# Feed-forward of a hybrid encoder block: residual scaling moved into the first group's loop, last norm's sums taken with the additions and its squares summed by ScalarE

## The chip, the cores and the metric

One core of one Trainium2 chip runs the whole kernel. The metric is the device time of one execution in microseconds (us); lower is better. The engines are called by the profile's names: PE (TensorE matmul), DVE (VectorE), ACT (ScalarE), POOL (GpSimd), SP (SyncE, which issues most DMAs). Each has its own queue of instructions and works through it strictly in order.

## The reference, cut to what matters

```
x = layer_norm(x, ln_in)                       # x: 1024 frames x 1024 features, float32
m = sigmoid(gate_A) * gMLP(x) + sigmoid(gate_B) * RWKV7(x)
x = layer_norm(ALPHA * x + m @ w_o, ln1_g, ln1_b)
gate, val = split(x @ w_up)                    # 2688 columns each
h = gelu(causal_conv3(gate) + conv_b) * val
x = layer_norm(ALPHA * x + h @ w_down, ln2_g, ln2_b)
```

The change concerns the last line: the residual `ALPHA * x`, the additions of `h @ w_down` to it, and the mean and variance of the norm over each frame's 1024 features.

## The kernel before, in words

The kernel does the token mixer first (some 1257 us), then the feed-forward part that the change touches. Matrix products are made in a split form: each float32 operand is a high part (name ending in h) and a low part (ending in l), and `mm3` makes three matmuls of them. The low part of every weight is a subtraction on POOL, the high part a cast on ACT; the raw weight comes by a DMA on the SP queue.

The feed-forward part (from line 1083) runs over 21 blocks of 128 columns of `w_up`, in 7 groups `g` of three blocks `f`. For each block PE makes the gate product for two halves `h` of the frames (into PSUM tiles `pu`, two buffers) and the value product for both halves (into `ps`, two buffers). The weights are `fuh`/`ful` (gate), `wh`/`wl` (value) and `fdh`/`fdl` (w_down). ACT copies the gate product to `gb` and scales it into `t`; DVE adds two shifted terms of the convolution; ACT applies gelu; DVE multiplies by the value product and casts to `th`; POOL makes the low part `tl`. When the three blocks of a group are made, PE multiplies them with `w_down` (PSUM tiles `pd`, four buffers) for 8 row tiles `n` of 128 frames and two halves `j` of 512 features, and DVE adds each `pd` into the residual `acc[n][j]`. The 16 residual tiles lie in buffers left over from earlier stages, so they appear under many names: f, sht, tv, acc, bvs, ff, gams, in the order of `n` (f, f for n=0 and 1; f, sht for 2; tv 3; acc 4; bvs 5; ff 6; gams 7).

Before the first additions the residual must be scaled: `load_bc(2)` fetches the gain and the bias of the norm before, broadcast to all partitions (tiles `bf`), ACT multiplies both by ALPHA, and a loop over the 16 tiles multiplies by the first (all on DVE) and adds the second (even `n` on POOL, odd on DVE). The buffers `bf` are used again for the last norm's gain and bias, so that load (`load_bc(4)`, issued on the ACT queue) waits until the scaling is over.

In the last group `finish(n, bc)` follows the additions of each row tile: `ln_stats` (line 346) reads both halves with BATCH_NORM_STATS and aggregates them on DVE, `rstd_of` (line 339) takes a square root on ACT and a reciprocal on DVE, and then half 0 is normalised by two DVE instructions, half 1 by one on ACT and two on POOL; the result goes out by DMA. For the last row tile the cut lies at 832 of 1024 features instead of 512.

The order on each engine: the token mixer is recorded and ordered by the kernel's own planner (class `Weave`); its instructions show as L279. The feed-forward part is issued directly, through the recording wrapper (they show as L92), and there the framework's scheduler decides the order on each engine.

Of the kernel before, what the change touches and what calls it, by code (L numbers as in the profile page):

```python
# [8 lines left out]
F32 = mybir.dt.float32  # L9
F32R = mybir.dt.float32r  # L10
AF = mybir.ActivationFunctionType
ALU = mybir.AluOpType
AX = mybir.AxisListType

P = 128
D = 1024
S = 1024
HT = 512
KT = 8
# [3 lines left out]
NF = FF // P  # L23
GRP = 3
# [259 lines left out]
def hybrid_block(ctx: ExitStack, tc, x, w_in, w_v, pars, rows, bs, ws, lor, w_o, w_up, w_dn, out):  # L284
# [7 lines left out]
    tiny = W.enter(ctx, tc.tile_pool(name="tiny", bufs=3), 3)  # L292
# [46 lines left out]
    def rstd_of(var, eps, scale=1.0, n=1, tag="rs"):  # L339
        s = tiny.tile([P, n], F32, name="rs_s", tag=tag + "s")  # L340
        A.activation(s, var, AF.Sqrt, bias=eps, scale=scale)
        r = tiny.tile([P, n], F32, name="rs_r", tag=tag + "r")
        V.reciprocal(r, s)
        return r

    def ln_stats(src):
        st = tiny.tile([P, 2, 6], F32, name="ln_st")
        for q in range(2):
            V.bn_stats(st[:, q, :], src[q] if isinstance(src, list) else src[:, q * HT:(q + 1) * HT])
        mv = tiny.tile([P, 2], F32, name="ln_mv")  # L350
        V.bn_aggr(mv, st)
        return mv, rstd_of(mv[:, 1:2], eps_ln)
# [212 lines left out]
    acc = [None] * KT  # L565
# [518 lines left out]
    with ExitStack() as st:  # L1084
        ep = st.enter_context
        gp = ep(pool("gp", 1))
        fw = ep(pool("fw", 2))
        fs = ep(pool("fs", 2))
        hp = ep(pool("hp", GRP + 1))
        ps_u = ep(pool("ps_u", 2, PSUM))  # L1090
        ps_d = ep(pool("ps_d", 4, PSUM))

        def load2(src, nm, bufs):
            wr = fw.tile([P, D], F32, name="wr2")
            SY.dma_start(wr, src)
            wh = fw.tile([P, D], F32R, name=nm + "h", bufs=bufs)
            wl = fw.tile([P, D], F32R, name=nm + "l", bufs=bufs)
            split(wh, wl, wr)
            return wh, wl

        def up(w, h, own=False):
            return gemm(w, h, xs=x1k(), ps=ps_u.tile([P, HT], F32, name="pu") if own else None)

        def load_bc(i0):
            bc = [fs.tile([P, D], F32, name=f"bf{i}", bufs=1) for i in range(2)]
            for i in range(2):
                A.dma_start(bc[i], rows[i0 + i:i0 + i + 1, :].partition_broadcast(P))
            return bc

        def finish(n, bc):  # L1110
            mv, r = ln_stats(acc[n])
            nm = tiny.tile([P, 1], F32, name="ln_nm", tag="rss")
            V.scalar_tensor_tensor(nm, mv[:, 0:1], -1.0, r, ALU.mult, ALU.mult)
            cut = HT if n < KT - 1 else 832
            whole = gams.rearrange("p a c t -> p (a c t)")
            for j, js in enumerate((slice(0, cut), slice(cut, D))):
                aj = acc[n][j] if n < KT - 1 else whole[:, js]
                if j:
                    A.activation(aj, aj, AF.Identity, bias=nm, scale=r)
                    G.tensor_tensor(aj, aj, bc[0][:, js], ALU.mult)  # L1120
                    G.tensor_tensor(aj, aj, bc[1][:, js], ALU.add)
                else:
                    V.scalar_tensor_tensor(aj, aj, mv[:, 0:1], bc[0][:, js], ALU.subtract, ALU.mult)
                    V.scalar_tensor_tensor(aj, aj, r, bc[1][:, js], ALU.mult, ALU.add)
                SY.dma_start(out[n * P:(n + 1) * P, js], aj)

        for g in range(NF // GRP):
            hh, hl, wd = [], [], []
            for f in range(g * GRP, (g + 1) * GRP):
                wg = load2(w_up[f], "fu", 2) if f else w0[0]  # L1130
                wv = load_w(0, w_up[NF + f]) if f else w0[1]
                wd.append(load2(w_dn[f * P:(f + 1) * P, :], "fd", GRP))
                th = hp.tile([P, S], F32R, name="th")
                tl = hp.tile([P, S], F32R, name="tl")
                gb = gp.tile([P, S + P + 104], F32, name="gb")
                G.memset(gb[:, 0:2], 0.0)
                cw = lambda i: par[:, C_CW + i * NF + f:C_CW + i * NF + f + 1]
                ts = []
                for h in range(2):
                    pg = up(wg, h, True) if f or h else up0[0]  # L1140
                    A.copy(gb[:, 2 + h * HT:2 + (h + 1) * HT], pg)
                    t0 = fs.tile([P, HT], F32, name="t0", bufs=3)
                    A.activation(t0, pg, AF.Identity, bias=par[:, C_CB + f:C_CB + f + 1], scale=cw(2))
                    V.scalar_tensor_tensor(t0, gb[:, 1 + h * HT:1 + (h + 1) * HT], cw(1), t0, ALU.mult, ALU.add)
                    V.scalar_tensor_tensor(t0, gb[:, h * HT:(h + 1) * HT], cw(0), t0, ALU.mult, ALU.add)
                    A.activation(t0, t0, AF.Gelu)
                    ts.append(t0)
                for h in range(2):
                    hs = slice(h * HT, (h + 1) * HT)
                    pv = up(wv, h) if f or h else up0[1]  # L1150
                    V.tensor_tensor(ts[h], ts[h], pv, ALU.mult)
                    V.tensor_copy(th[:, hs], ts[h])
                    G.tensor_tensor(tl[:, hs], ts[h], th[:, hs].bitcast(F32), ALU.subtract)
                hh.append(th)
                hl.append(tl)
            if g == 0:
                bc = load_bc(2)
                for i in range(2):
                    A.mul(bc[i], bc[i], ALPHA)
                for n in range(KT):  # L1160
                    for j in range(2):
                        js = slice(j * HT, (j + 1) * HT)
                        V.tensor_tensor(acc[n][j], acc[n][j], bc[0][:, js], ALU.mult)
                        (V if n % 2 else G).tensor_tensor(acc[n][j], acc[n][j], bc[1][:, js], ALU.add)
            if g == NF // GRP - 1:
                bc = load_bc(4)
            for n in range(KT):
                ns = slice(n * P, (n + 1) * P)
                for j in range(2):
                    js = slice(j * HT, (j + 1) * HT)  # L1170
                    po = ps_d.tile([P, HT], F32, name="pd")
                    for i in range(GRP):
                        mm3(po, hh[i][:, ns], hl[i][:, ns], wd[i][0][:, js], wd[i][1][:, js], i == 0, i == GRP - 1)
                    V.tensor_tensor(acc[n][j], acc[n][j], po, ALU.add)
                if g == NF // GRP - 1:
                    finish(n, bc)
    st_m.close()


# [61 lines left out]
```

## Time and profile before

| what | us |
|---|---|
| median of 3 runs (1964.23 to 1970.06) | 1964.5 |
| the profiled execution: its own time | 1965.61 |
| the profiled execution: its span | 1963.8 |
| PE busy in the span | 1854.9 (94%) |
| DVE, ACT, POOL busy | 994.2 (51%), 857.2 (44%), 916.0 (47%) |
| the feed-forward part, from about 1257 to the end | about 707 |

The span runs from the first to the last instruction of the profiled execution; 1.8 us of its own time lie around it. Busy shares are means over the whole span; the change touches two short stretches of it, the first 50 us of the feed-forward part and the last 44 us, and these are read in their own rows. Times in rows are from the span's start.

### The profile page before, as it was taken

The page shows a single profiled execution, that of the slowest core. Times are in us where ns is not written, and L with a number is a line of the kernel's source. Part 1 is how long each engine was busy: PE and PEld are TensorE (multiplying, and loading weights), DVE is VectorE, ACT ScalarE, POOL GpSimd, SP SyncE. Part 2 cuts the span into 40 slices and gives each one's busy share as a digit, 9 for nine tenths or more (in the row PEclk, how much of TensorE's full clock was granted, in tenths as well). Part 3 has the DMA queues.
Part 4 walks back from the last instruction along what each step waited for, and adds up shares of the span by engine and source line. Part 5 has one row for each costly group of instructions (what it writes and reads, how often), then busy time and mean ns, then how long its engine had stood idle before and what let it go on. Part 6 is the DMA issues. An engine that isn't in the chain of part 4 may idle for free.

```text
span 1963.8 us, 27242 instructions
## 1 busy us (share of the span) xinstructions
PE 1854.9 (94%) x10024; PEld 1499.5 (76%) x10024; DVE 994.2 (51%) x1806; ACT 857.2 (44%) x1733; POOL 916.0 (47%) x1505
## 2 busy tenths in 40 slices
PE   6997899999999999999998899989999999999997
PEld 5996677677777777777776677768888888888886
DVE  8423745666555567555554467683333332333327
ACT  5544465655556566556565565421212121212121
POOL 5202575557656565675548662272423232323224
PEclk9998999999999999999998999999999999999999
DMA  6112121111112122112131322231111111111102
GB/s 211 33 49 61 46 64 58 52 46 47 55 52 68 55 54 63 38 58 65 47 93 55 97 86 62 79 115 44 54 43 55 42 55 42 57 41 58 39 1 86
DMA packets 78884, 119.13 MB, mean 61 GB/s; under 512 B 27776, under 2 KB 47488, under 8 KB 78752
## 3 DMA queue, kind: packets, MB, share of 16 engines
q1 hardware_dynamic: 60640, 96.94, 16.3%
q10 hardware_dynamic: 18112, 20.45, 3.2%
q8 instruction: 80, 1.31, 0.3%
q14 instruction: 52, 0.43, 0.1%
HBM read 103.08 MB, written 14.29 MB: 60 GB/s over the span
## 4 chain that ended last, share of the span: by engine, by line
PE 64%; POOL 17%; DVE 9%; issue 4%; ACT 3%; DMA 2%; ACTq 1%; POOLq 0%; SPq 0%; DVEq 0%
PE ps L279 17%; PE ps L92 11%; PE pu L92 11%; PE pd L92 10%; PE pp L279 8%; POOL ydx L279 6%; POOL tm L279 6%; PE pv L92 4%; PE pc L279 2%; POOL wl L279 2%; POOL ar L279 1%; PE py L279 1%; DVE ln_st L92 1%; DVE vl L92 1%; DVE f L92 1%
## 5 line engine op out<-in xcount | busy, mean ns | idle before, releaser
L279 PE MATMUL ps<-xh,wh 128*128 128x512 f32 x896 | 373.4, 417 | 33.2 <-DVE tkr L279 13.1
L279 PE MATMUL ps<-xh,wl 128*128 128x512 f32 x896 | 369.2, 413 | 6.6 <-POOL wl L279 6.3
L279 PE MATMUL ps<-xlo,wh 128*128 128x512 f32 x896 | 373.3, 417 | 0.0
L279 PEld LDWEIGHTS ps<-xh,wh 128*128 128x128 f32 x896 | 173.4, 194 | 66.3 <-DVE tkr L279 14.6
L279 PEld LDWEIGHTS ps<-xh,wl 128*128 128x128 f32 x896 | 173.0, 193 | 37.3 <-POOL wl L279 8.3
L279 POOL TENSOR_TENSOR tm<-ydx,bd 128x60 f32<-128x60 f32 (+24 forms) x496 | 167.3, 337 | 67.4 <-DMA bd<-a_d 12.4
L279 PEld LDWEIGHTS ps<-xlo,wh 128*128 128x128 f32 x896 | 173.2, 193 | 29.0 <-issue 1.0
L279 POOL TENSOR_TENSOR wl<-wr,wh 128x1024 fp32r<-128x1024 f32 x50 | 122.3, 2445 | 149.7 <-ACT wh L279 130.3
L92 DVE SCALAR_TENSOR_TENSOR t<-gb,par,t 128x512 f32<-128x512 f32 x84 | 89.6, 1067 | 193.4 <-ACT t L92 192.0
L279 POOL TENSOR_TENSOR ydx<-ydx,tm 128x60 f32<-128x60 f32 (+24 forms) x496 | 167.0, 337 | 37.2
L279 DVE SCALAR_TENSOR_TENSOR bs<-pc,gams,sgm 64x64 f32<-64x64 f32 x240 | 67.9, 283 | 161.5 <-PE pc L279 159.2
L92 POOL TENSOR_TENSOR fdl<-wr,fdh 128x1024 fp32r<-128x1024 f32 x21 | 51.4, 2463 | 196.4 <-ACT fdh L92 196.4
L92 PE MATMUL pd<-fdh,th 128*128 128x512 f32 x336 | 130.7, 389 | 0.0
L92 PE MATMUL pd<-fdl,th 128*128 128x512 f32 x336 | 130.7, 389 | 0.0
L92 PE MATMUL pd<-fdh,tl 128*128 128x512 f32 x336 | 130.7, 389 | 0.0
L92 ACT CAST fdh<-wr 128x1024 fp32r<-128x1024 f32 x21 | 21.5, 1051 | 196.5 <-PE pd L92 182.7
L92 POOL TENSOR_TENSOR wl<-wr,wh 128x1024 fp32r<-128x1024 f32 x22 | 56.3, 2560 | 63.6 <-ACT wh L92 63.6
L92 POOL TENSOR_TENSOR ful<-wr,fuh 128x1024 fp32r<-128x1024 f32 x20 | 48.7, 2437 | 78.7 <-ACT fuh L92 72.9
L279 PEld LDWEIGHTS pp<-ar,bd 64*128 64x128 f32 x512 | 61.8, 189 | 27.6 <-issue 17.8
L279 ACT ACTIVATE sgm<-bs,gams 128x128 f32<-128x128 f32 x128 | 51.4, 401 | 71.1 <-DVE bs L279 67.6
L92 POOL TENSOR_TENSOR tl<-t,th 128x512 fp32r<-128x512 f32 x42 | 55.6, 1325 | 56.2 <-DVE th L92 56.2
L279 PE MATMUL pp<-ar,bd 64*128 64x128 f32 x512 | 74.8, 288 | 6.1 <-DVE ar L279 4.7
(356 smaller groups left out, 4460.8 us busy)
## 6 DMA issues: line engine op xcount, KB each, us to landing
wr<-in_dram SPq DMA_DIRECT2D x113, 512.0 KB
bd<-a_d SPq DMA_DIRECT2D x64, 128.0 KB
vraw<-in_dram SPq DMA_DIRECT2D x8, 528.0 KB
xt<-in_dram SPq DMA_DIRECT2D x8, 512.0 KB
v_d<-xt ACTq DMA_DIRECT2D x8, 512.0 KB
fv<-v_d ACTq DMA_DIRECT2D x16, 256.0 KB
f<-q_d SPq DMA_DIRECT2D x32, 128.0 KB
m_d<-gu ACTq DMA_DIRECT2D x14, 256.0 KB
```

The costliest lines, as they stand in the source:

```text
L92: return fn(*a, **k)
L279: fn(*a, **k)
```

## The change

Three edits in the feed-forward part.

1. The scaling of the residual moves from one loop of its own into the loop over row tiles of group 0. The multiplications of even `n` go from DVE to POOL, and all additions go to POOL.
2. In the last group the addition of `pd` also writes each row's sum (`accum_out`), as a SCALAR_TENSOR_TENSOR instruction.
3. `finish` makes the mean from the two sums with small instructions on one column, lets ACT square the deviations of both halves with a sum beside (Square, bias = minus the mean, `accum_out`), adds the two sums on DVE, and takes `rstd` from that. The two BATCH_NORM_STATS and the aggregation per row tile are gone.

```
-        def finish(n, bc):
-            mv, r = ln_stats(acc[n])
-            nm = tiny.tile([P, 1], F32, name="ln_nm", tag="rss")
-            V.scalar_tensor_tensor(nm, mv[:, 0:1], -1.0, r, ALU.mult, ALU.mult)
+        def finish(n, bc, s):
+            st = tiny.tile([P, 6], F32, name="fst", tag="ln_st")
+            V.tensor_scalar(st[:, 0:1], s[:, 0:1], s[:, 1:2], -1.0 / D, ALU.add, ALU.mult)
+            V.tensor_scalar(st[:, 1:2], st[:, 0:1], -1.0, None, ALU.mult)
+            for j in range(2):
+                sq = fs.tile([P, HT], F32, name="t0", bufs=3)
+                A.activation(sq, acc[n][j], AF.Square, bias=st[:, 0:1], accum_out=st[:, 2 + j:3 + j])
+            V.tensor_tensor(st[:, 4:5], st[:, 2:3], st[:, 3:4], ALU.add)
+            r = rstd_of(st[:, 4:5], eps_ln, scale=1.0 / D)
+            nm, mv = st[:, 5:6], st[:, 1:2]
+            V.tensor_tensor(nm, st[:, 0:1], r, ALU.mult)
...
-                for n in range(KT):
-                    for j in range(2):
-                        js = slice(j * HT, (j + 1) * HT)
-                        V.tensor_tensor(acc[n][j], acc[n][j], bc[0][:, js], ALU.mult)
-                        (V if n % 2 else G).tensor_tensor(acc[n][j], acc[n][j], bc[1][:, js], ALU.add)
...
             for n in range(KT):
                 ns = slice(n * P, (n + 1) * P)
+                s = tiny.tile([P, 2], F32, name="fsum", tag="rss")
                 for j in range(2):
                     js = slice(j * HT, (j + 1) * HT)
+                    if g == 0:
+                        (V if n % 2 else G).tensor_tensor(acc[n][j], acc[n][j], bc[0][:, js], ALU.mult)
+                        G.tensor_tensor(acc[n][j], acc[n][j], bc[1][:, js], ALU.add)
...
-                    V.tensor_tensor(acc[n][j], acc[n][j], po, ALU.add)
+                    if g < NF // GRP - 1:
+                        V.tensor_tensor(acc[n][j], acc[n][j], po, ALU.add)
+                    else:
+                        V.scalar_tensor_tensor(acc[n][j], po, 1.0, acc[n][j], ALU.mult, ALU.add, accum_out=s[:, j:j + 1])
                 if g == NF // GRP - 1:
-                    finish(n, bc)
+                    finish(n, bc, s)
```

How the scheduler places this is not in the diff. **POOL at the start of group 0**, before, from the first scaling addition to `ful`, the low part of the gate weight of the second block (wr_12795 is the raw w_down weight of the first block, wr_12873 the raw gate weight of the second; bf_13153 is the scaled gain, bf_13154 the scaled bias):

```order
L92 TENSOR_TENSOR f<-f,bf_13154 128x512 x3
L92 TENSOR_TENSOR fdl<-wr_12795,fdh 128x1024
L92 TENSOR_TENSOR sht<-sht,bf_13154 128x512
L92 TENSOR_TENSOR tl<-t_12806,th 128x512
L92 TENSOR_TENSOR ful<-wr_12873,fuh 128x1024
```

and after the change, the same stretch:

```order
L92 TENSOR_TENSOR f<-f,bf_13153 128x512 x3
L92 TENSOR_TENSOR sht<-sht,bf_13153 128x512
L92 TENSOR_TENSOR acc_3713<-acc_3713,bf_13153 128x512
L92 TENSOR_TENSOR f<-f,bf_13154 128x512 x5
L92 TENSOR_TENSOR sht<-sht,bf_13154 128x512
L92 TENSOR_TENSOR tv<-tv,bf_13154 128x512 x2
L92 TENSOR_TENSOR acc_3713<-acc_3713,bf_13154 128x512
L92 TENSOR_TENSOR acc_3714<-acc_3714,bf_13153 128x512
L92 TENSOR_TENSOR fdl<-wr_12795,fdh 128x1024
L92 TENSOR_TENSOR tl<-t_12806,th 128x512
L92 TENSOR_TENSOR ful<-wr_12873,fuh 128x1024
```

Fifteen scaling instructions instead of four now stand ahead of `ful` on POOL.

**ACT in the same stretch**, as a piece of the difference (the two `bf` DMAs are the load of the last norm's rows; wr_13025 is the raw w_down weight of the third block):

```order
 L92 CAST fuh<-wr_13013 128x1024
 L92 ACTIVATE t_12837<-t_12837 128x512
-L92 CAST wh<-wr 128x1024
+L92 DMA bf_16815<-in_dram 128x1024
+L92 CAST wh<-wr 128x1024
+L92 DMA bf_16816<-in_dram 128x1024
 L92 CAST fdh<-wr_13025 128x1024
-L92 DMA bf_16767<-in_dram 128x1024
-L92 DMA bf_16768<-in_dram 128x1024
 L92 COPY gb<-pu 128x512
```

The two loads stand one and two places earlier; the copy of the second block's gate product (`gb`), which frees PSUM for PE, is still behind both and now also directly behind a cast that needs wr_13025.

**DVE in the last group**, one row tile (n=4, names acc_3713 and acc_3714), before:

```order
L92 TENSOR_TENSOR acc_3714<-acc_3714,pd 128x512
L92 SCALAR_TENSOR_TENSOR tv<-tv,rs_r,bf_16768 128x512
L92 BN_STATS ln_st<-acc_3714 128x6
L92 TENSOR_TENSOR bvs<-bvs,pd 128x512
L92 BN_AGGR ln_mv<-ln_st 128x2
L92 BN_STATS ln_st<-bvs 128x6
L92 RECIPROCAL rs_r<-rs_s 128x1
L92 SCALAR_TENSOR_TENSOR acc_3713<-acc_3713,ln_mv,bf_16767 128x512
L92 SCALAR_TENSOR_TENSOR ln_nm<-ln_mv,rs_r 128x1
```

and after:

```order
L92 SCALAR_TENSOR_TENSOR acc_3714,fsum<-pd,acc_3714 128x512
L92 TENSOR_TENSOR fst<-fst,rs_r 128x1
L92 SCALAR_TENSOR_TENSOR tv<-tv,rs_r,bf_16816 128x512
L92 TENSOR_SCALAR fst<-fsum 128x1
L92 TENSOR_SCALAR fst<-fst 128x1
L92 SCALAR_TENSOR_TENSOR acc_3713<-acc_3713,fst,bf_16815 128x512
L92 TENSOR_TENSOR fst<-fst 128x1
L92 SCALAR_TENSOR_TENSOR bvs,fsum<-pd,bvs 128x512
L92 RECIPROCAL rs_r<-rs_s 128x1
L92 SCALAR_TENSOR_TENSOR bvs,fsum<-pd,bvs 128x512
```

In the second list `TENSOR_TENSOR fst<-fst,rs_r` is the shift `nm` of the tile before, and `TENSOR_TENSOR fst<-fst` adds the two sums of squares; the additions of the next tile (`bvs,fsum<-pd,bvs`) stand behind it, where before one of them stood ahead of the aggregation.

## Rows read from the trace of the kernel before

**Rows 1.** The page's first section, and the busy time of each engine in two stretches of the feed-forward part (stretch, length, PE, PEld, DVE, ACT and POOL busy us with instructions, granted PE clock, DMA share, GB/s).

```profile
PE 1854.9 (94%) x10024; PEld 1499.5 (76%) x10024; DVE 994.2 (51%) x1806; ACT 857.2 (44%) x1733; POOL 916.0 (47%) x1505
...
1500.00:1600.00 100.00, 100.00 (x443) 82.81 (x442) 31.16 (x43) 20.99 (x28) 30.06 (x19) 1.00 0.17 53
1920.00:1964.00 44.00, 32.61 (x144) 26.66 (x143) 38.01 (x74) 8.62 (x16) 22.50 (x17) 0.92 0.26 96
```

**Rows 2.** Timeline of PE in group 0, around its two waits (start us, us, engine, line, what, in brackets the idle time before and what ended it).

```profile
1278.05 0.39 PE L92 MATMUL pu<-x1la,fuh 128*128 128x512 f32 x1
1280.67 0.50 PE L92 MATMUL pu<-x1ha,ful 128*128 128x512 f32 x1 [2.23 <-POOL ful L92]
...
1303.51 0.39 PE L92 MATMUL ps<-x1hb,wl 128*128 128x512 f32 x1
1308.89 0.79 PE L92 MATMUL pu<-x1ha,fuh 128*128 128x512 f32 x1 [4.99 <-ACT t L92]
```

**Rows 3.** Busy time by stretch again, columns as in rows 1: a stretch in the token mixer that begins 2.29 us after a wait of 7.49 us, and two stretches behind the first wait of rows 2.

```profile
1066.20:1069.70 3.50, 3.50 (x11) 2.71 (x10) 1.47 (x1) 0.00 (x0) 3.42 (x3) 0.50 0.44 150
...
1281.30:1284.70 3.40, 3.40 (x10) 2.67 (x9) 3.40 (x5) 0.53 (x1) 2.25 (x2) 0.52 0.51 154
1284.70:1288.10 3.40, 3.40 (x16) 2.76 (x15) 3.40 (x2) 0.52 (x1) 3.40 (x2) 0.98 0.07 11
```

**Rows 4.** The chain that ended last, the gate product of the third block of group 0 and of the first of group 1 (start us, us, what): 48 matmuls each.

```profile
1308.89 12.69 PE pu L92 x48
...
1365.10 10.88 PE pu L92 x48
```

**Rows 5.** Timeline of POOL in group 0: with DVE at work beside it, and from 1312 with DVE mostly waiting; last, a group of the same kind of 128x512 instruction with float32 output (count, busy us, mean ns).

```profile
1265.06 3.37 POOL L92 TENSOR_TENSOR f<-f,bf 128x512 f32<-128x512 f32 x2 [7.45 <-ACT bf L92]
1271.89 2.86 POOL L92 TENSOR_TENSOR fdl<-wr,fdh 128x1024 fp32r<-128x1024 f32 x1
1277.83 2.79 POOL L92 TENSOR_TENSOR ful<-wr,fuh 128x1024 fp32r<-128x1024 f32 x1
1312.21 2.40 POOL L92 TENSOR_TENSOR ful<-wr,fuh 128x1024 fp32r<-128x1024 f32 x1 [5.73 <-issue]
1317.08 1.30 POOL L92 TENSOR_TENSOR tl<-t,th 128x512 fp32r<-128x512 f32 x1 [0.89 <-DVE th L92]
1333.40 2.56 POOL L92 TENSOR_TENSOR wl<-wr,wh 128x1024 fp32r<-128x1024 f32 x1 [2.39 <-ACT wh L92]
...
L279 POOL TENSOR_TENSOR acc<-acc,bx 128x512 f32<-128x512 f32 x2 | 2.6, 1282 | 0.1
```

**Rows 6.** Timeline of DVE and ACT in group 0 (ACTq is ACT's DMA queue).

```profile
1263.03 1.29 DVE L92 TENSOR_TENSOR f<-f,bf 128x512 f32<-128x512 f32 x2
1274.95 6.82 DVE L92 TENSOR_TENSOR tv<-tv,bf 128x512 f32<-128x512 f32 x4
...
1261.78 1.09 ACT L92 ACTIVATE bf<-bf 128x1024 f32<-128x1024 f32 x1
1278.30 1.04 ACT L92 CAST fdh<-wr 128x1024 fp32r<-128x1024 f32 x1 [3.68 <-DMA wr<-in_dram]
1304.37 3.10 ACTq L92 DMA_DIRECT2D bf<-in_dram  x2
1307.57 0.59 ACT L92 COPY gb<-pu 128x512 f32<-128x512 f32 x1 [9.57 <-DVE gams L92]
```

**Rows 7.** Timelines of DVE, ACT and POOL in the last group, one round of the row tiles.

```profile
1941.26 0.15 DVE L92 SCALAR_TENSOR_TENSOR ln_nm<-ln_mv,rs_r 128x1 f32<-128x1 f32 x1
1941.33 0.67 DVE L92 TENSOR_TENSOR acc<-acc,pd 128x512 f32<-128x512 f32 x1
1941.93 0.74 DVE L92 SCALAR_TENSOR_TENSOR tv<-tv,rs_r,bf 128x512 f32<-128x512 f32 x1
1944.57 1.18 DVE L92 SCALAR_TENSOR_TENSOR acc<-acc,ln_mv,bf 128x512 f32<-128x512 f32 x1
1945.67 0.14 DVE L92 SCALAR_TENSOR_TENSOR ln_nm<-ln_mv,rs_r 128x1 f32<-128x1 f32 x1
...
1941.45 0.82 ACT L92 ACTIVATE tv<-tv,ln_nm,rs_r 128x512 f32<-128x512 f32 x1 [1.48 <-DVE ln_nm L92]
...
1942.34 2.86 POOL L92 TENSOR_TENSOR tv<-tv,bf 128x512 f32<-128x512 f32 x2 [1.55 <-ACT tv L92]
```

**Rows 8.** The same small shift instruction where POOL is at work (first of each pair DVE, then the POOL instruction it lies beside).

```profile
1243.78 1.02 DVE L279 SCALAR_TENSOR_TENSOR ln_nm<-ln_mv,rs_r 128x1 f32<-128x1 f32 x1
1242.39 2.38 POOL L279 TENSOR_TENSOR wl<-wr,wh 128x1024 fp32r<-128x1024 f32 x1 [47.50 <-ACT wh L279]
...
1957.96 1.03 DVE L92 SCALAR_TENSOR_TENSOR ln_nm<-ln_mv,rs_r 128x1 f32<-128x1 f32 x1
1955.52 3.45 POOL L92 TENSOR_TENSOR ff<-ff,bf 128x512 f32<-128x512 f32 x2 [1.54 <-ACT ff L92]
```

**Rows 9.** Groups of ACT instructions that price the squares (count, busy us, mean ns, idle before).

```profile
L279 ACT ACTIVATE f<-f,half 128x512 f32<-128x512 f32 x16 | 11.5, 721 | 0.3
L92 ACT ACT_TABLE_LOAD x24 | 30.8, 1283 | 3.9 <-DVE xt L92 2.3 <-PEq L1231 1.2
```

**Rows 10.** The end: DVE's first addition of the last row tile, and its last instruction.

```profile
1952.01 0.67 DVE L92 TENSOR_TENSOR gams<-gams,pd 128x512 f32<-128x512 f32 x1
...
1958.91 1.07 DVE L92 SCALAR_TENSOR_TENSOR gams<-gams,rs_r,bf 128x832 f32<-128x832 f32 x1
```

## The prediction

> **What bounds the kernel now.** The page's first section comes first: PE is busy 94% of the span, so most of the kernel is matmuls back to back [rows 1]. The change adds no matmul and takes none away, so it can only move the time where PE waits or where the end hangs on another engine. The windows show where that is. In the middle of the feed-forward part PE is busy 100 of 100 us [rows 1], and a delay that arises before it is carried through to the end unchanged. In the last 44 us PE is busy for 32.6. PE's timeline has two waits in group 0: one for the low weight `ful` from POOL, whose next matmul starts 2.62 us after the last one instead of 0.23, and one of 5.15 us for ACT [rows 2]. Behind the first the granted clock reads 0.52 for 3.4 us, its lower level of 1.2 GHz, and then 0.98 [rows 3]; behind the second, 48 matmuls take 12.69 us instead of 10.88 [rows 4].
>
> The second wait has its cause on ACT: the copy that frees `pu` stood idle behind the two `bf` loads in ACT's queue, which waited until DVE had done the last scaling of gams [rows 6].
>
> In the last group one round of a row tile takes 4.41 us on DVE, from one shift `ln_nm` to the next [rows 7], while PE makes two `pd` in 4.08 us (18 matmuls of 0.227 us, one piece of 10.88 us having 48 [rows 4]). I read the round as a closed chain: shift at 1941.26, ACT's normalisation at 1941.45, POOL's two instructions from 1942.34 to 1945.20, then DVE's SCALAR_TENSOR_TENSOR, started at 1944.57 but 1.18 us long instead of 0.74, ending half a microsecond after POOL did, and the next shift at 1945.67 [rows 7]. DVE and POOL do not work side by side there: a DVE instruction with two SBUF inputs waits for a POOL instruction to end. It holds even for one column: the shift of 0.15 us takes 1.02 and 1.03 where POOL is at work, and both times it ends within 0.03 us of POOL's end [rows 8].
>
> **Part 1: the scaling (group 0).** DVE loses 8 multiplications and 8 additions, POOL gets these 16 besides its 8. What counts is what stands in POOL's queue ahead of `ful`, for which PE already waits: fifteen 128x512 instructions instead of four, then `fdl`, `tl` and `ful`. POOL can start at 1262.9, when ACT has scaled the first row (1261.78 + 1.09) [rows 6]. A 128x512 instruction on POOL takes 1.68 us (3.37 for two) beside a DVE instruction of the contending kind, 1.28 alone [rows 5]. In that stretch DVE has 13 of these (8 multiplications, 4 convolution terms, one cast), so I take 13 x 1.68 + 2 x 1.28 = 24.4, and the rest alone: 2.40 + 1.30 + 2.40 = 6.1 [rows 5]. `ful` ends at 1293.4, against 1277.83 + 2.79 = 1280.6 now. Bounds: all alone, 15 x 1.28 + 6.1, gives 1288.2; all beside DVE, 25.2 + 7.4 (2.86, 1.73 as two instructions of its kind, 2.79), gives 1295.5. I take 13 of 15 because DVE's list is long enough for it.
>
> The Trainium skill, SBUF — State Buffer, Who interferes with whom, says that of the two the one that comes second is blocked for the whole instruction of the other. By that a pair would cost 1.28 + 0.60 = 1.88 us, and `ful` would end another 13 x 0.20 = 2.6 us later; the row's 1.68 decides.
>
> From `ful` on PE has 94 matmuls of this block left, 94 x 0.227 = 21.3 us. Behind a long wait the clock costs more: after the wait of 7.49 us the lower level still stood 5.8 us after PE's restart [rows 3], a loss of 2.9; after a short wait 1.7 (half of 3.4). I take 2.4. PE is then ready for the third block at 1293.4 + 21.3 + 2.4 = 1317.1. Does the second wait stay? Behind `ful` POOL has six 128x512 (7.7), `wl` (2.56), three more (3.8), `fdl` (2.40), all alone: 16.5. That frees the buffer of wr_13025; from the end of an `fdl` (1274.75) to the cast of the next load (1278.30) it takes 3.55, the cast 1.04, and from the copy's start to PE's restart 1.32 [rows 2, 5, 6]. Together 22.4, so 1315.8: 1.3 us before PE needs it. The second wait goes, unless that load, beside the two `bf` loads, comes over 1.3 us later. `wl` needs no wait: it is ready 10.3 us after `ful`, and PE needs it after 46 x 0.227 + 2.4 = 12.8.
>
> Before, the third block began at 1308.89 and lost 1.81 to the clock, as good as a start at 1310.70. So part 1 costs 1317.1 - 1310.7 = **+6.4 us** (bounds: +0.5 with 1288.2 and a clock loss of 1.7; +9 with 1295.5 and 2.9). DVE's shorter list gains nothing there, since nobody on PE's path waits for it any more.
>
> **Parts 2 and 3: the last norm.** Per tile DVE loses two BATCH_NORM_STATS (0.6 from start to start) and the aggregation, some 1.3 us. But DVE's sum does not set the round, the chain does, and the new order makes it longer. New round: shift to normalisation on ACT 0.19, to POOL 0.89, POOL's first 1.28, DVE's SCALAR_TENSOR_TENSOR 0.66, POOL's second 1.28, then the addition of the two square sums, a two-input instruction of one column that I expect to wait for POOL as the shift does [rows 8], 0.12; and now both additions of the next tile, 0.60 each, and a reciprocal 0.07 stand behind it, ahead of the next shift (an addition is priced from 1941.33 to 1941.93, a small instruction from 1941.26 to 1941.33) [rows 7]. Sum 5.7, less some 0.1 of overlap: 5.6 instead of 4.4, **+1.2 a round**. The squares don't lie on it: ACT needs 0.72 each [rows 9], from 0.2 us after the sums on, and is done before POOL's first instruction ends or soon after.
>
> The first two tiles have no POOL work yet: there squares (2 x 0.72 for 1.4 of statistics) are even, and the one ACT_TABLE_LOAD that now follows them costs 1.28 [rows 9], with the later first round some +1.6. Five rounds then give +6.0. In the last tile squares cost 1.44 against statistics and aggregation, but its two additions follow at once, and from its first addition to the last DVE instruction I count 7.1 instead of 8.0 (1952.0 to 1959.98 [rows 10]): -0.9. Together +6.7. The written sums have no price in this trace: between nothing (the same addition from PSUM, 0.67) and a small instruction each, 0.15 [rows 7]. I take 0.07, twice a round: +0.3 over what the rounding above holds. **+7 us**, bounds 0 (the small addition doesn't wait, round 4.3 to 4.5) and +8.5.
>
> The Trainium skill, VectorE: DVE Perf Modes, Two Vector instructions with no wait between them, says that an instruction which also writes out its accumulator is two, the second reading it out. By that the upper end of the sums' price would hold, and part 2 would give about +8; no run here shows it yet.
>
> **Sum.** 6.4 + 7 = +13.4. The profiled execution took 1965.6 and would take 1979; its own time is 1.1 above the median, so against the median of 1964.5 I forecast **1978 us**, 0.7% slower. A change of under 0.3%, 5.9 us, can't be told from none.
>
> **Rivals.**
> - *Only the scaling costs.* The addition of one column on DVE doesn't wait for POOL, for instance since it is a TENSOR_TENSOR and the rows show a SCALAR_TENSOR_TENSOR. The round stays at 4.3 to 4.5, the tail within 1 us, and the sum is +7: 1971.5. Against it: 128x512 TENSOR_TENSORs wait for POOL too (6.82 us for four beside POOL, 0.65 each without [rows 6]). Chance 0.18.
> - *Only the tail costs.* POOL is as fast as alone, `ful` ends near 1288, the lost second wait pays for the longer first one: +0.5 to +2, and with the tail +8: 1972.5. Chance 0.06.
> - *Not slower.* The mechanism is the one exchange in group 0, with a tail that costs nothing: POOL's longer queue makes one wait of about 10 us of two that cost 2.4 + 1.7 and 5.15 + 1.8 = 11 now. It decides at `ful`: if that ends before 1289 and the round stays under 4.5, the sum is 0 to +2, and I give 1966. For it: 1.28 alone. Against it: every row of POOL beside DVE's list. Chance 0.12.
> - *Faster.* DVE's relief lets the tail run at PE's 4.08 (7 x 0.33 = 2.3 us) and both waits go (11 us): 1952. `ful` would have to end by 1278.3, which fifteen instructions ahead of it exclude even at 1.28. Chance 0.04, for what I don't see.
>
> That the change isn't made as told can be left out: the order lists show fifteen scalings ahead of `ful`, and one table load in the last group.
>
> **How the numbers follow.** Forecast 0.60, the rivals 0.18, 0.06, 0.12, 0.04. Slower by over 0.3% holds the forecast, the second rival and most of the first: 0.80. Within 0.3%: the third and a rest of the first, 0.16. Faster 0.04. The range for 8 in 10 leaves out the third rival and the fastest, and goes from the low side of the first, 1968, to both upper bounds less what is unlikely together (+9 and +8.5 give 1982), with 2 us more for a second wait that stays after all: 1984.
>
> **What would show it.** Right: in group 0 one PE wait of 13 to 17 us for `ful`, ending near 1293, no wait for ACT behind it or a short one, and the first `pd` 5 to 8 us later; in the tail a round of some 5.6 us, with `fst<-fst` taking 1 us or more beside POOL. Wrong: a PE wait of under 11 us there, a round of under 4.7, or squares that DVE waits for while POOL is idle.

## The result, and the profile after

The change makes the kernel slower: 1978.71 us (median of 7 runs, 1974.56 to 1986.35) against 1966.67 (7 runs of the kernel before beside them, 1964.23 to 1970.06), a ratio of 1.0064 with a 95% interval of 1.0049 to 1.0078, or +9.6 to +15.3 us. The forecast was 1978.0 in 1968 to 1984. The profiled execution took 1978.71, its span is 1976.8, against 1965.61 and 1963.8.

First the page's first section of the kernel after and the busy times by stretch (stretch, length, PE, PEld, DVE, ACT, POOL, PE clock, DMA share, GB/s), which answer to [rows 1].

```profile
PE 1858.4 (94%) x10024; PEld 1504.4 (76%) x10024; DVE 974.8 (49%) x1806; ACT 868.5 (44%) x1765; POOL 931.4 (47%) x1521
...
1250.00:1300.00 50.00, 34.62 (x148) 27.99 (x147) 30.31 (x30) 16.78 (x26) 38.41 (x24) 0.86 0.22 74
1300.00:1350.00 50.00, 50.00 (x222) 41.45 (x221) 21.09 (x22) 13.15 (x18) 34.03 (x22) 1.00 0.38 116
1350.00:1450.00 100.00, 100.00 (x442) 82.85 (x442) 30.91 (x42) 20.35 (x27) 29.90 (x18) 1.00 0.16 48
```

DVE's work fell by 19.4 us and the kernel became slower. All of group 0's loss now lies before 1300, the middle is as full as it was, and the rest has to be in the tail.

Group 0 in the kernel after, answering to [rows 2, 5, 6]: PE at its one wait, the chain behind it (start, us, what), then POOL's and ACT's timelines.

```profile
1279.08 0.39 PE L92 MATMUL pu<-x1la,fuh 128*128 128x512 f32 x1
1294.03 0.80 PE L92 MATMUL pu<-x1ha,ful 128*128 128x512 f32 x1 [14.56 <-POOL ful L92]
```

```profile
1294.03 12.66 PE pu L92 x46
1306.69 10.88 PE ps L92 x48
1317.57 10.88 PE pu L92 x48
1328.45 10.88 PE ps L92 x48
1339.33 5.89 PE pd L92 x26
```

```profile
1263.97 4.70 POOL L92 TENSOR_TENSOR f<-f,bf 128x512 f32<-128x512 f32 x3 [5.34 <-ACT bf L92]
...
1272.03 8.52 POOL L92 TENSOR_TENSOR f<-f,bf 128x512 f32<-128x512 f32 x5
...
1288.13 2.33 POOL L92 TENSOR_TENSOR fdl<-wr,fdh 128x1024 fp32r<-128x1024 f32 x1
1290.42 1.26 POOL L92 TENSOR_TENSOR tl<-t,th 128x512 fp32r<-128x512 f32 x1
1291.64 2.34 POOL L92 TENSOR_TENSOR ful<-wr,fuh 128x1024 fp32r<-128x1024 f32 x1
...
1314.25 1.05 ACT L92 CAST fdh<-wr 128x1024 fp32r<-128x1024 f32 x1 [5.68 <-DMA wr<-in_dram]
1315.20 0.58 ACT L92 COPY gb<-pu 128x512 f32<-128x512 f32 x1
1315.68 0.79 ACT L92 ACTIVATE t<-pu,par 128x512 f32<-128x512 f32 x1
```

POOL works through fifteen scalings from 1263.97 to 1288.13, then the three instructions down to `ful`, which ends at 1293.98. PE stands for 14.56 us, and the second wait is gone: the third block starts at 1317.57, where the 48th matmul of `ps` ends.

One round of the last group, answering to [rows 7]: DVE, then POOL.

```profile
1945.58 0.15 DVE L92 TENSOR_TENSOR fst<-fst,rs_r 128x1 f32<-128x1 f32 x1
1945.65 0.74 DVE L92 SCALAR_TENSOR_TENSOR f<-f,rs_r,bf 128x512 f32<-128x512 f32 x1
...
1947.40 1.17 DVE L92 SCALAR_TENSOR_TENSOR tv<-tv,fst,bf 128x512 f32<-128x512 f32 x1 [0.70 <-ACT t L92]
1948.49 1.24 DVE L92 TENSOR_TENSOR fst<-fst 128x1 f32<-128x1 f32 x1
1949.65 0.68 DVE L92 SCALAR_TENSOR_TENSOR acc<-pd,acc 128x512 f32<-128x512 f32 x1
1950.26 0.08 DVE L92 DVE_READ_ACCUMULATOR acc<-pd,acc 128x1 f32 x1
...
1950.93 0.15 DVE L92 TENSOR_TENSOR fst<-fst,rs_r 128x1 f32<-128x1 f32 x1
...
1946.72 3.00 POOL L92 TENSOR_TENSOR sht<-sht,bf 128x512 f32<-128x512 f32 x2 [2.36 <-ACT sht L92]
```

The round is 5.35 us (1945.58 to 1950.93) where it was 4.41. The addition of two columns takes 1.24 and ends with POOL's pair, at 1949.73 and 1949.72. Both additions of the next tile stand behind it.

**How the kernels are compared.** PE's transposes of gams, the last piece of the token mixer, start at another time in each profiled run: between 1258.3 and 1265.8 in the nine kernels whose tiles lie as before. One execution's start says little by itself, since it moves by several us from run to run. So each profile is cut in two stretches: **A** from that start to the first addition of the last group on DVE, and **B** from there to the end of DVE's last instruction. The starts are rows of each kernel's timeline; ratios are to the kernel before, run on the same chip.

| kernel | ratio (95%) | transposes | first addition | A | B |
|---|---|---|---|---|---|
| before | | 1258.26 | 1922.05 | 663.79 | 37.93 |
| after | 1.0064 (1.0049 to 1.0078) | 1259.29 | 1928.93 | 669.64 | 43.99 |
| e1 scaling alone | 1.0026 (1.0014 to 1.0038) | 1260.37 | 1930.59 | 670.22 | 37.93 |
| e2 norm alone | 1.0037 (1.0024 to 1.0050) | 1260.99 | 1924.73 | 663.74 | 44.00 |
| e3 one-input addition | 1.0032 (1.0020 to 1.0044) | 1264.30 | 1934.57 | 670.27 | 38.68 |
| e6 norm, one input | 1.0006 (0.9993 to 1.0018) | 1265.75 | 1929.57 | 663.82 | 38.70 |
| e5 low parts on DVE | 1.0047 (1.0031 to 1.0063) | 1258.32 | 1927.25 | 668.93 | 38.69 |
| e7 late scaling | 1.0065 (1.0046 to 1.0083) | 1269.55 | 1939.07 | 669.52 | 38.70 |
| e8 late, old engines | 1.0014 (1.0002 to 1.0027) | 1266.41 | 1926.89 | 660.48 | 38.68 |
| e10 rows late | 0.9989 (0.9975 to 1.0003) | 1261.39 | 1923.61 | 662.22 | 37.97 |
| e11 shift later | 0.9985 (0.9973 to 0.9996) | 1274.14 | 1926.97 | 652.83 | 40.43 |
| e12 early square root | 1.0049 (1.0033 to 1.0065) | 1272.66 | 1937.19 | 664.53 | 40.44 |
| e13 shift later, plain | 0.9958 (0.9946 to 0.9970) | 1265.32 | 1918.17 | 652.85 | 38.71 |
| e14 one column more | 1.0030 (1.0017 to 1.0043) | 1264.50 | 1929.08 | 664.58 | 37.93 |

The change costs 5.85 in A and 6.06 in B, 11.9 us together. The other 1.03 us of the two spans' 13.0 lie ahead of the transposes.

### The profile page after: what moved, and what is told of

Read it like the earlier page. It is cut to its first block, busy times and chain, and to the rows that moved or that the text cites. A ratio compares the mean times of both kernels' runs of the same rounds, so it can differ in the third digit from the quotient of the medians.

```text
span 1976.8 us, 27299 instructions
## 1 busy us (share of the span) xinstructions
PE 1858.4 (94%) x10024; PEld 1504.4 (76%) x10024; DVE 974.8 (49%) x1806; ACT 868.5 (44%) x1765; POOL 931.4 (47%) x1521
## 4 chain that ended last, share of the span: by engine, by line
PE 67%; POOL 18%; DVE 6%; issue 4%; ACT 3%; DMA 2%; ACTq 0%; SPq 0%; POOLq 0%; DVEq 0%
PE ps L279 18%; PE ps L92 11%; PE pu L92 11%; PE pd L92 10%; PE pp L279 8%; POOL tm L279 6%; POOL ydx L279 6%; PE pv L92 4%; PE pc L279 2%; POOL wl L279 2%; POOL ar L279 1%; PE py L279 1%; DVE vl L92 1%; POOL f L92 1%; DVE ln_st L92 1%
## 5 line engine op out<-in xcount | busy, mean ns | idle before, releaser
L279 PEld LDWEIGHTS ps<-xh,wh 128*128 128x128 f32 x896 | 173.9, 194 | 66.0 <-DVE tkr L279 14.6
L92 DVE TENSOR_TENSOR t<-t,ps 128x512 f32<-128x512 f32 x42 | 28.9, 687 | 110.2 <-PE ps L92 96.8
```

The lines of the kernel that those rows point to most:

```text
L92: return fn(*a, **k)
L279: fn(*a, **k)
```

## The experiments

**e1, e2: each part alone.** e1 takes the lines of the last norm back (`finish`, the column `s`, the last group's additions that write sums) and keeps the scaling in the loop. e2 takes the scaling back and keeps the new norm; its edit to the changed kernel is

```diff
             if g == 0:
...
+                for n in range(KT):
+                    for j in range(2):
...
+                        V.tensor_tensor(acc[n][j], acc[n][j], bc[0][:, js], ALU.mult)
+                        (V if n % 2 else G).tensor_tensor(acc[n][j], acc[n][j], bc[1][:, js], ALU.add)
...
-                    if g == 0:
-                        (V if n % 2 else G).tensor_tensor(acc[n][j], acc[n][j], bc[0][:, js], ALU.mult)
-                        G.tensor_tensor(acc[n][j], acc[n][j], bc[1][:, js], ALU.add)
```

> The change's first part alone: the scaling inside the loop and on POOL, the last norm as before. Theory (fifteen scalings stand ahead of `ful` in POOL's queue; the changed kernel's trace has the first `pd` 5.8 us later once the mixer's own 1.03 us is taken off): 5 to 7 us above the kernel before, so about 1972.5; one PE wait for `ful` of 13 to 16 us, no second wait, and a last-group round of 4.4 us. Rival (the two parts depend on one another and the time arises in the tail alone): within 1.5 us of the kernel before.

> The change's other two parts alone: the sums with the additions and the squared deviations on ACT, the scaling as before. Theory: the time arises in the last group's round, 5.35 us instead of 4.41, and is independent of group 0: 6 to 7 us above the kernel before, about 1973, with PE's two waits in group 0 as before. Rival (the longer tail only shows because group 0 ended later): under 2 us.

Measured: e1 costs 5.1 us (2.8 to 7.5), with A +6.43, B as before to the hundredth and one PE wait for `ful` of 14.6 us; e2 costs 7.3 (4.7 to 9.8), with A as before, B +6.07 and PE's two waits of 2.3 and 5.0 us as before. The two parts don't touch one another, and their sum by the ratios, 12.4, is the change's 12.6. Both theories held, both rivals fell.

**e3, e6: the addition with one tensor input.** e3 is the changed kernel, e6 is e2, both with this line:

```diff
-            V.tensor_tensor(st[:, 4:5], st[:, 2:3], st[:, 3:4], ALU.add)
+            V.tensor_scalar(st[:, 4:5], st[:, 2:3], st[:, 3:4], None, ALU.add)
```

> The changed kernel with one instruction in another form: the addition of the two sums of squares is a TENSOR_SCALAR (the second sum is its scalar operand), so it has one tensor input instead of two; same place in DVE's queue, same operands. Theory (a DVE instruction with two tensor inputs from SBUF waits until POOL's instruction has ended, even for one column, and the next tile's additions stand behind it): it takes 0.1 to 0.2 us instead of 1.24, the round falls from 5.35 to 4.3 to 4.6 and the time by 5 to 7 us, to about 1972.5. Rival A (the addition is late because ACT's second square is late): it starts and ends as before, no change, 1978.7. Rival B (DVE meets the same wait at its next instruction with two tensor inputs, `nm` or the addition): the round stays above 5.1, under 2 us gained.

> The last norm's new form with the one-input addition, and the scaling as in the kernel before. Theory (the two costs add up, and the tail's is that one wait and 1.6 us in its first two tiles): 0 to 2 us above the kernel before, 1967 to 1969. Rival A (late squares): as the norm alone, about 1973. Rival B (DVE's 1.3 us less a tile become a gain once the wait is gone: the round falls to PE's 4.1): 1 to 3 us below the kernel before.

The same round in e3, DVE and then POOL:

```profile
1948.76 0.20 DVE L92 TENSOR_SCALAR fst<-fst 128x1 f32<-128x1 f32 x1
1948.88 0.68 DVE L92 SCALAR_TENSOR_TENSOR tv<-pd,tv 128x512 f32<-128x512 f32 x1
...
1950.16 0.15 DVE L92 TENSOR_TENSOR fst<-fst,rs_r 128x1 f32<-128x1 f32 x1
...
1954.47 0.15 DVE L92 TENSOR_TENSOR fst<-fst,rs_r 128x1 f32<-128x1 f32 x1
...
1948.37 1.62 POOL L92 TENSOR_TENSOR f<-f,bf 128x512 f32<-128x512 f32 x1
```

The addition now takes 0.20 us and lies in the middle of a POOL instruction (1948.37 to 1949.99). The next tile's addition of 512 columns, one of whose two inputs is in PSUM, lies beside it too and takes its 0.68 us. Every instruction stands at the same place in every queue as in the changed kernel. So rival A, a late second square, fell: the addition is early once its form is another. The round is 4.31, B falls by 5.31 in e3 and 5.30 in e6. That is the tail's cost but for some 0.77 us. The B rivals fell too: the round stays neither above 5.1 nor falls to PE's 4.1; DVE's shorter list makes it 0.1 us shorter than before, no more. I read the chain that remains as shift, ACT, POOL's first instruction, DVE's scaling beside it and the additions behind; no run tests that. In total e3 costs 6.3 us (3.9 to 8.7), e6 1.2 (-1.4 to 3.5).

**e5: the second block's low parts on DVE.** On top of e3 (`load2` hands its new last argument on to `split`, which picks the engine of the low part by it):

```diff
-                wg = load2(w_up[f], "fu", 2) if f else w0[0]
-                wv = load_w(0, w_up[NF + f]) if f else w0[1]
+                wg = load2(w_up[f], "fu", 2, "v" if f == 1 else "g") if f else w0[0]
+                wv = load_w(0, w_up[NF + f], "v" if f == 1 else "g") if f else w0[1]
```

> The changed kernel with the one-input addition, and the second block's two low weights `ful` and `wl` on DVE instead of POOL; POOL keeps all 24 scalings. Theory (PE waits because `ful` stands behind fifteen scalings in POOL's queue): DVE, whose list is shorter now, makes `ful` some 8 us earlier (about 1285 instead of 1294), PE's wait falls from 14.6 to about 5.5 us, and the time is 5 to 8 us below the kernel with the one-input addition alone (ratio 1.0032), so within 3 us of the kernel before. Rival (another cause holds PE there: the load, ACT's cast or the transposes' end): the wait stays above 12 us, no gain.

PE's waits in group 0 of e5 (us in total, times, longest), and behind them ACT's timeline there:

```profile
PE pu L92 <- ACT t L92: 5.3, 1, 5.3
PE pu L92 <- DVE ful L92: 5.3, 1, 5.3
```

```profile
1310.48 1.04 ACT L92 CAST fdh<-wr 128x1024 fp32r<-128x1024 f32 x1 [9.87 <-DMA wr<-in_dram]
1311.43 0.58 ACT L92 COPY gb<-pu 128x512 f32<-128x512 f32 x1
```

The wait for `ful` shrank to 5.3 us as the theory has it, but a second wait of 5.3 came: A is 1.34 shorter than in e3, not 5 to 8. I had the mechanism and missed what is late next. POOL's list also holds `fdl`, which frees the buffer of a load; ACT's cast of that load, and behind it the copy that frees `pu`, come at 1311. In the changed kernel this path ended 1.1 us ahead of PE (1315.68 + 0.79 against 1317.57). The ratio of e5 is 3.3 us above what A and B give (5.9). The profiled execution is the fastest of its seven, 8.1 us below their median; where the rest of 3.3 lies stays open.

**e10: the last group's rows later.** The kernel before with

```diff
+                if after is not None:
+                    V.tensor_copy(bc[i][:, 0:1], after)
                 A.dma_start(bc[i], rows[i0 + i:i0 + i + 1, :].partition_broadcast(P))
...
-                bc = load_bc(4)
+                bc = load_bc(4, acc[KT - 1][1][:, 0:1])
```

> The kernel before with one edit: the last group's two rows are loaded only after the group before it, so the two loads no longer stand in ACT's queue in group 0. Theory (they hold the copy that frees `pu`, and with it PE, for 5.15 us and 1.8 us of clock): the second wait goes, the first stays, 5 to 7 us below the kernel before. Rival (the copy waits for DVE or for another cause that the profile hides): no change, within 1 us.

PE's waits in e10, and ACT's timeline:

```profile
PE pu L92 <- ACT t L92: 2.9, 1, 2.9
PE pu L92 <- POOL ful L92: 2.3, 1, 2.3
```

```profile
1301.05 0.58 ACT L92 COPY gb<-pu 128x512 f32<-128x512 f32 x1
...
1311.71 0.63 ACT L92 ACTIVATE t<-t 128x512 f32<-128x512 f32 x1 [9.40 <-DVE t L92]
1312.25 1.03 ACT L92 CAST fuh<-wr 128x1024 fp32r<-128x1024 f32 x1
1313.18 0.58 ACT L92 COPY gb<-pu 128x512 f32<-128x512 f32 x1
```

The loads did hold the first copy (now 1301.05, with the transposes 3.13 us later than in before, where it was 1307.57). But the next copy stands behind the third block's gelu, which waits for DVE's convolution, and that for the last scalings. So 1.6 us of A are gained where 5 to 7 were expected, and the ratio gives -2.2 (-4.9 to 0.6), which can't be told from none. The theory held for the first half of the block alone: 2.9 us of the wait of 5.0 have another cause than the two loads.

**e7, e8: the scaling behind the second block's low parts.** The rows' factor is made from `wl`, so the scalings can't start before it; e7 keeps the changed kernel's engines, e8 those of the kernel before. Both have e10's edit and the one-input addition.

```diff
+                if f == 1:
+                    after = wv[1][:, 0:1].bitcast(F32)
...
+                al = tiny.tile([P, 1], F32, name="fal", tag="ln_nm")
+                V.tensor_scalar(al, after, 0.0, ALPHA, ALU.mult, ALU.add)
                 for i in range(2):
-                    A.mul(bc[i], bc[i], ALPHA)
+                    A.mul(bc[i], bc[i], al)
```

> The changed kernel with the one-input addition and the same 24 scalings on POOL and 8 on DVE, but the scaled rows wait for the second block's `wl` (the factor is taken from it), so the scalings stand behind `ful` and `wl` in POOL's queue; the last group's two rows are loaded only after the group before it. Theory (the place in POOL's queue costs, not the instructions as such): the wait for `ful` falls from 14.6 to under 1 us. But the 24 POOL instructions, 1.3 to 1.7 us each from about 1287 on, now stand ahead of the third block's `tl`, which the first `pd` needs near 1326: a new wait of some 10 us there, so only 3 to 9 us gained on the kernel with the one-input addition, about 1964 to 1970. Rival A (POOL is done by then): 15 to 17 us gained, about 1957. Rival B (the wait for `ful` has another cause): it stays, no gain.

> As the kernel with the late scaling, but with the engines of the kernel before (DVE 16 multiplications and 8 additions, POOL 8 additions). Theory (PE's two waits of group 0 and the clock behind them, 11 us in the trace of before, all come from the scaling's place and from the two row loads that wait for it in ACT's queue): no wait above 1 us between the transposes and the first `pd`, some 10 us below the kernel before, about 1957, the last group's round 4.3 us as in the kernel with the one-input addition. Rival (DVE's 24 instructions, behind which the second block's casts and the third block's convolution now stand, become a wait before the first `pd`): 0 to 5 us below the kernel before.

PE's waits and one instruction of POOL in e7, then PE's waits in e8:

```profile
PE pd L92 <- DVE th L92: 8.9, 1, 8.9
PE pd L92 <- POOL tl L92: 4.9, 1, 4.9
...
1337.47 0.10 POOL L92 MEMSET gb<- 128x2 f32 x1
```

```profile
PE ps L92 <- DVE t L92: 5.1, 1, 5.1
```

In both the wait for `ful` is gone, so it was the place in POOL's queue. In e7 two others came, ahead of `pd` and 13.8 us together, and A is only 0.75 below e3, where 3 to 9 us were expected. POOL's 24 instructions now stand ahead of the second block's `tl` (4.9 us). They also stand ahead of a MEMSET that writes two border columns of the third block's `gb`; DVE's convolution of that block stands 15.94 us for it, starts at 1337.60, and so `th` is late (8.9 us). In e8 DVE's 24 hold the product that frees `ps`; A is 3.3 below before. Here the rival had the mechanism. Rivals A and B of e7 fell. As a whole e8 costs 2.8 us (0.4 to 5.3), although A and B together gain 2.6, and e7 12.8 where they cost 6.5: 5.3 and 6.3 us are neither in A nor in B.

**e11, e12: a version meant to beat both, and an early square root.** Only the multiplications stay in group 0; the second row's additions move to groups 1 to 4. e11 has it with e10's edit, the one-input addition and one square root ahead of the norm; e12 is e6 with the square root alone.

```diff
                     if g == 0:
-                        (V if n % 2 else G).tensor_tensor(acc[n][j], acc[n][j], bc[0][:, js], ALU.mult)
-                        G.tensor_tensor(acc[n][j], acc[n][j], bc[1][:, js], ALU.add)
+                        V.tensor_tensor(acc[n][j], acc[n][j], bc[0][:, js], ALU.mult)
...
                         V.tensor_tensor(acc[n][j], acc[n][j], po, ALU.add)
+                        if g == 1 + n // 2:
+                            V.tensor_tensor(acc[n][j], acc[n][j], bc[1][:, js], ALU.add)
...
+                A.activation(tiny.tile([P, 1], F32, name="fsq", tag="ln_nm"), ts[1][:, 0:1], AF.Sqrt, bias=eps_ln, scale=0.0)
```

> A version meant to beat both: in group 0 only the 16 multiplications of the scaling, all on DVE, none on POOL; the 16 additions of the second row move to groups 1 to 4 (four each, on DVE, right behind the addition of `pd`); the last group's rows are loaded after the group before it; last norm as in the changed kernel with the one-input addition, and one square root on ACT ahead of it, which draws the table load forward. Theory (POOL's and DVE's lists in group 0 held `ful` and the convolution, and DVE and POOL held one another): no PE wait above 1.5 us from the transposes to the first `pd`, that stretch 8 to 11 us shorter than in the kernel before (663.8 us from the transposes of gams to the last group's first addition), and a tail of about 37.4 us, so 7 to 11 us below the kernel before. Rival A (the 16 multiplications alone still keep the second block's convolution from DVE, and PE waits as in the kernel with the late scaling): 2 to 5 us below. Rival B (the additions moved delay `pd` in groups 1 to 4): PE below 100% there, gain lost.

> The new norm with the one-input addition on the scaling of the kernel before, and one square root on ACT right after the last product, ahead of the first squares, so that the ACT_TABLE_LOAD of 1.28 us runs while PE still makes the first `pd`. Theory (the load stood on the first round's path): the tail, from the first addition to the last DVE instruction, falls from 38.70 to about 37.4 us, so the time is within 1 us of the kernel before. Rival (the first rounds wait for PE's `pd` anyway): 38.7, as without.

e11's A is 652.83, 10.96 us shorter than before, with no PE wait behind the transposes: all that group 0 had lost. But the ratio gives only 3 us (0.8 to 5.3). The square root was a miss: DVE in e12's first rounds shows why.

```profile
1942.57 0.16 DVE L92 RECIPROCAL rs_r<-rs_s 128x1 f32<-128x1 f32 x1
1942.77 0.16 DVE L92 TENSOR_TENSOR fst<-fst,rs_r 128x1 f32<-128x1 f32 x1
1942.84 0.74 DVE L92 SCALAR_TENSOR_TENSOR f<-f,rs_r,bf 128x512 f32<-128x512 f32 x1
1943.51 0.68 DVE L92 SCALAR_TENSOR_TENSOR f<-pd,f 128x512 f32<-128x512 f32 x1
```

The root is ready earlier, and the program's order then puts shift and scaling of one tile ahead of the second addition of the next. The sums, and with them the squares, come later, and B grows by 1.74 us (e12 against e6) instead of falling by 1.3. In total e12 costs 9.7 us (6.5 to 12.8), where within 1 was expected. Without the root, in e13 below, B is 38.71 again.

**e13, e14: the rest.** In e7, e8, e11 and e12 the ratio lies 5.3 to 6.4 us above what A and B give; in the others it lies between 1.3 below and 1.9 above, but for e5's 3.3. The four have one thing in common: a new tile of 128x1. e13 is e11 without the square root, and so without that tile. e14 is the kernel before with

```diff
-            nm = tiny.tile([P, 1], F32, name="ln_nm", tag="rss")
+            nm = tiny.tile([P, 1], F32, name="ln_nm")
```

> As the version with the additions of the second row in groups 1 to 4, without the early square root and so without its column (the one new tile of 128x1 that shifts the addresses of the tiles behind it). Theory (that kernel lost its 11 us of group 0 elsewhere: 1.7 in the tail, since the early square root drew the shift ahead of the second addition, and some 5 us in the token mixer, which comes later in all four kernels that have a new column): the stretch from the transposes of gams to the last group's first addition stays near 653, the tail goes back to 38.7, the mixer to that of the kernel before, so 8 to 11 us below the kernel before, about 1959. Rival (the mixer's end comes later for another cause): 3 to 6 us below.

> The kernel before, every instruction the same and in the same order on every engine; only the last norm's shift `ln_nm` has a column of its own instead of one that it shares, which moves the addresses of the tiles allocated behind it. Theory (those addresses cost the mixer time): 4 to 7 us above the kernel before, none of it behind the transposes of gams. Rival (the later mixer of the four kernels is chance or has another cause): within 1.5 us.

e14 costs 5.9 us (3.3 to 8.5) with no instruction changed or moved. 0.8 of it is in A (the wait for ACT is 5.8 us where it was 5.0), none in B. That leaves 5.1 us ahead of the transposes. Groups of PE's instructions in the first 1240 us (count, busy us, mean ns of one, idle before), of before and then of e14:

```profile
L279 PE MATMUL ps<-xlo,wh 128*128 128x512 f32 x878 | 366.2, 417 | 0.0
L92 PE MATMUL pv<-vh,xlo 128*128 128x352 f32 x192 | 62.0, 323 | 0.0
```

```profile
L279 PE MATMUL ps<-xlo,wh 128*128 128x512 f32 x871 | 366.9, 421 | 0.0
L92 PE MATMUL pv<-vh,xlo 128*128 128x352 f32 x192 | 62.7, 327 | 0.0
```

The same matmuls take 4 ns more, 1%. For the second of these groups 327 stands in all five kernels with the new tile and 323 in all nine without it; the first has 421 to 423 in the five and 417 to 419 in the nine. Over the whole span PE is busy 1865.2 to 1871.3 us in the five and 1854.9 to 1864.5 in the nine. The granted clock isn't the cause: it is 0.978 to 0.981 in e14's seven runs and 0.977 to 0.981 in those of before beside them, and other groups keep their time (`pp<-wst,fv`, 128 matmuls, 277 ns in both). What the edit changes is where tiles lie, so I put the loss down to addresses; none of these rows shows an address. e13 has neither the tile nor the loss: the chain in group 0 is PE without a gap,

```profile
1285.05 10.88 PE pu L92 x48
1295.93 10.88 PE ps L92 x48
1306.81 10.88 PE pu L92 x48
1317.69 10.88 PE ps L92 x48
1328.57 11.56 PE pd L92 x51
```

A is 652.85, B 38.71, and the kernel takes 1956.8 us (median of 11) against 1966.08: **8.3 us faster than before (5.9 to 10.6)**, which A and B give as 10.2. It beats both kernels.

## Why the prediction was right

- **The second wait goes, the first grows.** Right: one wait of 14.56 us (forecast 13 to 17), none for ACT behind it. Fifteen scalings took 24.16 us (24.4), `fdl`, `tl` and `ful` 5.85 (6.1), so `ful` ends at 1293.98, or 1292.95 with the transposes' 1.03 us taken off (1293.4). The slower clock behind the wait cost 12.66 - 46 x 0.227 = 2.2 us (2.4). That is less than the 2.9 which the prediction read behind a wait half as long, so "behind a long wait the clock costs more" isn't borne out here. The third block starts at 1317.57 - 1.03 = 1316.54, 5.84 us behind 1310.70 (+6.4). e1 shows this part alone at +5.1 in the ratio and +6.43 in A.
- **The nearness of the total.** 1978.71 against 1978.0 is partly luck. The forecast added 13.4 to a median of 1964.5; the kernel before took 1966.67 beside the changed one, and the change is 12.6 by the ratio, 11.9 by A and B.
- **Contention on POOL.** Five scalings took 8.52, 1.70 each, beside DVE. By the Trainium skill (SBUF — State Buffer, Who interferes with whom: the second of the two is blocked for the whole of the first) I had estimated 1.88; this trace doesn't agree, and the row's 1.68 was the better guide.
- **The ACT path with 1.3 us of margin.** Right: 1.1. e5 shows that it decides as soon as `ful` comes earlier. The cause that the prediction gave for the second wait of the kernel before, the two `bf` loads, is half of it: without them e10 still waits 2.9 us for ACT.
- **The tail: +7, measured +6.06.** Right in mechanism, e3 and e6 show it: the column addition waits for POOL. By the prediction's terms: up to the shift of the third tile +1.84 (+1.6); from there to the last tile's first addition +4.89 (+6.0); the last tile -0.67 (-0.9). The mis-sized term is the round, 5.35 instead of 5.6: POOL's pair took 3.00 us with DVE's instruction between, not 1.28 + 0.66 + 1.28 = 3.22.
- **The written sums, 0.07 each.** Each is a second instruction, DVE_READ_ACCUMULATOR, of 0.08 us. The Trainium skill (VectorE: DVE Perf Modes, Two Vector instructions with no wait between them) says that there are two, and this trace agrees. The upper price of 0.15, which the prediction hung on that, does not hold, and a tail of +8 with it.
- **The rivals.** "Only the scaling costs" fell because a TENSOR_TENSOR of one column waits as the SCALAR_TENSOR_TENSOR did; e3 is the kernel that this rival described, and it costs 6.3 us, where +7 was given. "Only the tail costs" fell because POOL was not as fast as alone: fifteen scalings took 24.16 us, not 15 x 1.28 = 19.2, and e1, which leaves the tail as it was, costs 5.1. "Not slower" had its point at 1289, which `ful` missed by 4 us.
- **What the prediction didn't say.** DVE's relief was called worthless; that holds for this program's order. e13 shows that the stage had 11 us to give, once the second row's additions leave group 0 and the last group's rows are loaded late.

## What to carry to other kernels

Before work is moved to an engine that is "only half busy", look for the one instruction in its queue that the bound engine waits for, and count what will stand ahead of it; when that wait is taken away, name what is late next, since in four of these kernels (e5, e7, e8, e10) another wait took its place. In a chain that runs over two engines, an instruction of one column in the wrong form can cost as much as one of 512. Compare kernels by stretches between fixed points of one trace as well as by the total: one more small tile, with no instruction changed, can hide a gain of the same size.

## What the runs showed of the hardware

- A DVE instruction with two tensor inputs from SBUF waits for a POOL instruction to end even for one column (1.24 us in the kernel after); the same sum with one tensor input and a scalar operand takes 0.20 beside POOL (e3).
- One more tile of 128x1, with the same instructions in the same order, changed the pace of matmuls by 1% (323 to 327 ns, 417 to 421) and the kernel's time by 5.9 us (e14). That it is the addresses is argued, not shown; which tile's place does it, and why, stays open.
- ACT's accumulator is read by an instruction of its own too, ACTIVATION_READ_ACCUMULATOR, 0.18 to 0.19 us in e6 and e12, of which the next square hides half (in e6 it starts at 1933.29, the next square at 1933.38).
